# Queries projected by Wq times transposed Wk, formed on the chip, against unprojected keys: the mLSTM part of a hybrid encoder layer

## The chip, the cores and the metric

One Trainium2 chip, of which the kernel uses 1 core. The metric is the device time of one execution in microseconds (us), the median of several runs. The engines are PE (TensorE: PE the matmuls, PEld its weight loads), DVE (VectorE), ACT (ScalarE), POOL (GpSimd) and SP (SyncE, which issues most transfers). Each runs its own list of instructions in order; semaphores make one wait for another.

## The reference, cut to what matters

One encoder layer for 1024 tokens of width 1024, all float32. Two token mixers (a chunkwise mLSTM and an RG-LRU, each in two directions) run side by side, are merged by gates, and a product-key expert mixer (PEER) and a norm follow. The change touches the mLSTM alone, which has 4 heads of width 256:

```python
xc = silu(dwconv_centred(xm, conv_w, conv_b)).reshape(B, S, H, d)
q = einsum("bshd,hde->bhse", xc, w_q)
k = einsum("bshd,hde->bhse", xc, w_k) / sqrt(d)        # d = 256, so / 16
v = einsum("bshd,hde->bhse", xv, w_v)
# one direction, chunks of 128 tokens, carry (C, n, m):
s   = einsum("bhtd,bhsd->bhts", qc, kc) * w_intra
num = w_inter * einsum("bhtd,bhde->bhte", qc, C) + einsum("bhts,bhse->bhte", s, vc)
den = w_inter * einsum("bhtd,bhd->bht", qc, n) + sum(s)
kw  = kc * w_state
C   = decay * C + einsum("bhsd,bhse->bhde", kw, vc)
n   = decay * n + sum(kw)
```

The key k meets nothing but the query q: in the scores s, and through C and n, which are sums over keys. Nothing else reads either.

## The kernel before, in words

The work has these stages, by the clock of the profiled execution: the first norm, the projections and the RG-LRU (0 to about 397 us, the first mLSTM block among them), the four mLSTM heads one after the other (about 397 to 923 us), the merge of the two branches (923 to about 1100 us), the expert mixer's queries and its top-k searches (about 1100 to 1750 us), and then the dense stage with the gathers of expert rows (to the end). Products of two float32 values are mostly formed as three matmuls in the type float32r on split operands: `split` writes a high part (on ACT, line 78) and the remainder (on DVE or POOL, line 71), and `mm3` issues the three matmuls (lines 84, 85 and 86). A matmul of plain float32 tiles, without a split, shows in the trace as two PE records.

For one head the parts are these.

- `ml_x` projects two blocks of 128 channels, convolves them on DVE (line 321) and forms xc, which it splits into a high and a low tile.
- `ml_qkv` forms q and k: per head 2 x 2 x 2 groups of 6 matmuls 128x512 into a PSUM tile `pg`, each group moved out by one ACT activation (line 582). Its weights, 128x1024 with Wq in the left half and Wk in the right, come through a list of weight loads (`ws_plan`, `ws_get`): a raw tile `wr` (three buffers), a high tile `wh` from ACT and a low tile `wl` from POOL. Then it forms v in 48 matmuls 128x256.
- `ml_e` loads rows of exponents, masks them on POOL (line 619) and takes 16 exponentials on ACT (line 621).
- `ml_core` begins with the scores, plain float32 matmuls of k with q (line 638), and transposes of k (line 647). Then it works through 8 chunks in both directions; the states C and n go through DVE (line 685), ACT and POOL.
- `ml_out` normalises and transposes back (line 729), and multiplies into the gate tile on DVE (line 731).

Between the chunks of a head's core stand the projections that don't depend on it ("fill": the output gate of the head and the merge gates, 24 matmuls 128x512 per PSUM tile `ps`, with operand tiles `h`). Which instruction stands where on an engine is set by a scheduler that orders the program as it is built, by its own list of priorities; so a change in one place can move instructions in others.

SBUF tiles named `u` come from a pool of 18 tiles of 128x1032 float32; a name such as `u_2696` is a tile, `pg_2697` a PSUM tile, and the numbers run in order of their allocation.

Of the kernel before, what the change touches and what calls it, by code (L numbers as in the profile page):

```python
# [8 lines left out]
F32 = mybir.dt.float32  # L9
F32R = mybir.dt.float32r  # L10
# [3 lines left out]
AF = mybir.ActivationFunctionType  # L14
OP = mybir.AluOpType
# [7 lines left out]
H = 4  # L23
# [11 lines left out]
class K:  # L35
# [506 lines left out]
    def ml_x(self, h, done=None):  # L542

        nc = self.nc
        st = {}
        st["xm"], st["xc"] = [], []
        for e in range(2):
            blk = 2 * h + e
            x = self.pad_proj(blk, done if e == 0 else None)
            hi, lo = self.u(F32R), self.u(F32R)  # L550
            self.split(x[:, 2:2 + S], hi[:, :S], lo[:, :S])
            st["xm"].append((hi, lo))
            xc = self.u()
            self.conv(xc, x, V_MCW, V_MCB, blk)

            def act(xc=xc):
                nc.scalar.activation(xc[:, :S], xc[:, :S], AF.Silu)
                hi, lo = self.u(F32R), self.u(F32R)
                self.split(xc[:, :S], hi[:, :S], lo[:, :S])
                st["xc"].append((hi, lo))  # L560

            if e == 0:
                act()
            else:
                self.later = act
        return st

    def ml_qkv(self, h, st):
        nc = self.nc
        wh, wl = self.ws_get(("qk", h))  # L570
        for i, nm in enumerate(("q", "k")):
            st[nm] = []
            for e in range(2):
                t = self.u()
                for hf in range(2):
                    c = slice(hf * 512, hf * 512 + 512)
                    p = self.psg()
                    for cb in range(2):
                        o = i * 512 + cb * 256 + e * 128
                        self.mm3(p, (wh[:, o:o + 128], wl[:, o:o + 128]),  # L580
                                 (st["xc"][cb][0][:, c], st["xc"][cb][1][:, c]), cb == 0, cb == 1)
                    nc.scalar.activation(t[:, c], p, AF.Copy, scale=1.0 if i == 0 else 1.0 / 16.0)
                st[nm].append(t)
        wh, wl = self.ws_get(("v", h))
        st["v"] = []
        for g in range(2):
            vh, vl = (self.u(F32R).rearrange("p (c e) -> p c e", e=258) for _ in range(2))
            one = self.ones[:, 0:8].rearrange("p (c e) -> p c e", e=2)
            nc.gpsimd.tensor_copy(vh[:, :, 256:257], one[:, :, 0:1])
            self.sub("p", vh[:, :, 257:258], one[:, :, 0:1], one[:, :, 0:1])  # L590
            self.sub("p", vl[:, :, 256:258], one, one)
            for c in range(4):
                t = slice((g * 4 + c) * 128, (g * 4 + c) * 128 + 128)
                p = self.psg()
                for cb in range(2):
                    xh, xl = st["xm"][cb]
                    w = slice(cb * 256, cb * 256 + 256)
                    self.mm3(p[:, 0:256], (xh[:, t], xl[:, t]), (wh[:, w], wl[:, w]), cb == 0, cb == 1)
                nc.scalar.activation(vh[:, c, 0:256], p[:, 0:256], AF.Copy)
                self.sub("v", vl[:, c, 0:256], p[:, 0:256], vh[:, c, 0:256].bitcast(F32))  # L600
            st["v"].append((vh, vl))
        del st["xm"], st["xc"]
# [5 lines left out]
    def col(self, t, d, c, h):  # L608
        i = d * 32 + c * 4 + h
        return t[:, i:i + 1]  # L610
# [137 lines left out]
    def mixer_plan(self):  # L748
        plan = []
        inw = lambda b, e=WENG: plan.append((("in", b), [(self.A["win"][b], 1024)], 1024, e))  # L750
        lru = lambda n: plan.append((("lru", n), [(self.A["lwr"][n], 256), (self.A["lwi"][n], 256)], 512, "pd"))
        for n in range(NB + 1):
            if n == 1:
                lru(n - 1)
            inw(16 + n if n < NB else 0, "pd")
            if n in LRU_MG:
                inw(32 + LRU_MG.index(n))
            if n > 1:
                lru(n - 1)
            inw(24 + n if n < NB else 1, "pd")  # L760
            if n == 0:
                inw(48, "pd")
        seq = []
        mg = iter(range(len(LRU_MG), 16))
        m = lambda n: [("mg", next(mg)) for _ in range(n)]
        seq += m(MG[0])
        for h in range(H):
            for o in MLSEQ:
                if o == "m":
                    seq += m(1)  # L770
                elif o == "core":
                    seq += [(o, h)] + [m(1)[0] if f == "m" else ("o", h) for f in COREF[h]] + [("end", h)]
                elif o == "x":
                    seq += [("x", h + 1)] if h < H - 1 else m(LASTM)
                else:
                    seq += [(o, h)]
        seq += [("mg", i) for i in mg]
        for s_ in seq:
            if s_[0] == "x":
                inw(2 * s_[1])  # L780
                inw(2 * s_[1] + 1)
            elif s_[0] == "o":
                inw(8 + 2 * s_[1])
                inw(9 + 2 * s_[1])
            elif s_[0] == "mg":
                inw(32 + s_[1])
            elif s_[0] == "qkv":
                h = s_[1]
                plan.append((("qk", h), [(self.A["mwq"][h], 512), (self.A["mwk"][h], 512)], 1024, WENG))
                plan.append((("v", h), [(self.A["mwv"][h], 512)], 512, WENG))  # L790
        self.ws_plan(plan)
        self.seq = seq
# [741 lines left out]
WENG = "p"  # L1534
# [17 lines left out]
def host(**i):  # L1552
    f = lambda a: np.ascontiguousarray(a)
    a = {k: np.asarray(v) for k, v in i.items()}
    x = a["x"][0]
    d = {}
    d["xT"] = f(x.T.reshape(8, 128, S))
    w = a["w_in"][0]
    blk = lambda m: f(m.reshape(m.shape[0] // 128, 128, m.shape[1] // 128, 128).transpose(2, 1, 0, 3).reshape(
        m.shape[1] // 128, 128, m.shape[0]))  # L1560
    d["win"] = blk(np.concatenate([w[:, :2048], w[:, 2064:], w[:, 2048:2064], np.zeros((D, 112), np.float32)], axis=1))
    hw = lambda m: f(m[0].reshape(H, 2, 128, 256).transpose(0, 2, 1, 3).reshape(H, 128, 512))
    d["mwq"], d["mwk"], d["mwv"] = hw(a["mlstm_w_q"]), hw(a["mlstm_w_k"]), hw(a["mlstm_w_v"])
    lw = lambda m: f(m[0].transpose(1, 2, 0, 3).reshape(8, 128, 256))
    d["lwr"], d["lwi"] = lw(a["lru_w_r"]), lw(a["lru_w_i"])
    col = lambda v: v.reshape(-1, 128).T
    d["pvec"] = f(np.concatenate([
        col(a["norm1_g"][0]), col(a["mlstm_conv_w"][0]), col(a["mlstm_conv_b"][0]), col(a["mlstm_norm_g"][0]),
        col(a["lru_conv_w"][0]), col(a["lru_conv_b"][0]), col(a["lru_b_r"][0]), col(a["lru_b_i"][0]),
        col(a["lru_lambda"][0]), col(a["norm2_g"][0]),  # L1570
        np.concatenate([a["b_gates"][0], np.zeros(112, np.float32)])[:, None]], axis=1))
    d["bm"], d["bl"], d["wo"], d["wq"] = (blk(a[n][0]) for n in ("w_branch_mlstm", "w_branch_lru", "w_out", "peer_w_q"))
    d["keys"] = f(a["peer_sub_keys"][0].reshape(4, 4, 128, 128).transpose(0, 3, 1, 2).reshape(4, 128, 512))
    d["pu"], d["pv"] = f(a["peer_u"][0]), f(a["peer_v"][0])
    d["u5"] = f(a["peer_u"][0].reshape(128, 128, 8, 128).transpose(1, 3, 2, 0).reshape(128, 128, 1024))
    d["v5"] = f(a["peer_v"][0].reshape(128, 128, 1024).transpose(1, 0, 2))
    d["fg"] = f(a["final_norm_g"])
    d["g2"] = f(a["norm2_g"][0])
    return d
# [14 lines left out]
```

## Time and profile before

| what | value |
|---|---|
| median of 3 runs | 3574.14 us (3574.14, 3561.7, 3575.13) |
| the profiled execution, its own time | 3566.02 us |
| its span (first to last instruction) | 3563.9 us |
| mean granted TensorE clock, share of full speed | 0.969 |
| busy in the span | PE 94%, PEld 79%, DVE 82%, ACT 39%, POOL 48% |
| the four heads' stretch, 397 to 923 us | PE busy 484.5 of 526.0 us |

Every row of the trace is one execution's. A timeline row gives the start of a group of equal instructions and the time to the end of the last; matmuls overlap, so the cost of one in a row of many is the distance between starts, not the duration that stands beside it.

### The profile page before, as it was taken

Reading aid. Unit: us, or ns where it says so; the run is one execution under the profiler, and the core shown is the slowest. Engines: PE = TensorE matmul, PEld = TensorE weight load, DVE = VectorE, ACT = ScalarE, POOL = GpSimd, SP = SyncE. Lnnn points to the kernel's source line nnn. Section 1 sums busy time; section 2 is a strip of 40 time slices with the busy share of each in tenths; the row PEclk is TensorE's granted clock in tenths of the full one; section 3 lists DMA queues with packets and bytes.
Section 4 is the critical chain, followed back from the end, with each engine's and each line's share of the span. In section 5 each row is a group of like instructions: output and inputs, shape, how many; then the busy total and the mean of one; then the engine's idle time right before and its main releaser. Section 6 shows DMA issues by size and latency. Waiting matters only on the chain. (4 is left out here: it accounts for less than half of the span.)

```text
span 3563.9 us, 48538 instructions
## 1 busy us (share of the span) xinstructions
PE 3343.9 (94%) x17633; PEld 2827.0 (79%) x17633; DVE 2929.6 (82%) x5279; ACT 1392.0 (39%) x2565; POOL 1713.4 (48%) x1336
## 2 busy tenths in 40 slices
PE   7999999899899899878899999999999999999998
PEld 5787788778685565556788888998888999999987
DVE  8777574674327866998899999989999999999998
ACT  4565655655120240233333333343333334333333
POOL 7445354444102322342455555655555665666663
PEclk9999999999999999989899999999999999999999
DMA  2122211111466575558888879997887999999996
GB/s 107 60 71 68 72 51 51 63 48 44 154 217 208 159 251 199 174 170 258 312 318 301 283 275 342 360 338 276 314 284 279 341 357 351 344 347 334 352 348 239
DMA packets 319665, 812.56 MB, mean 228 GB/s; under 512 B 25600, under 2 KB 137408, under 8 KB 319424
## 3 DMA queue, kind: packets, MB, share of 16 engines
q0 software_dynamic: 115200, 419.48, 32.4%
q1 hardware_dynamic: 115184, 333.21, 26.7%
q10 hardware_dynamic: 89040, 56.76, 5.3%
q8 instruction: 138, 2.26, 0.3%
q14 instruction: 103, 0.84, 0.1%
HBM read 726.35 MB, written 83.00 MB: 227 GB/s over the span
## 5 line engine op out<-in xcount | busy, mean ns | idle before, releaser
L1334 POOL DMA_INDIRECT k<-in_pv,k x384 | 514.0, 1338 | 378.6 <-DVE k L1365 182.3
L1334 POOL DMA_INDIRECT k<-in_pu,k x384 | 506.6, 1319 | 332.7 <-DVE k L1357 148.0
L84 PE MATMUL ps<-h2h,wh 128*128 128x320 f32 x2048 | 637.2, 312 | 10.2 <-DVE u L1268 9.9
L85 PE MATMUL ps<-h2l,wh 128*128 128x320 f32 x2048 | 635.2, 310 | 0.0
L86 PE MATMUL ps<-h2h,wl 128*128 128x320 f32 x2048 | 628.9, 310 | 5.8 <-DVE wl L71 5.8
L851 PE MATMUL ps<-u,wr 128*128 128x384 f32 (+1 forms) x1920 | 581.1, 460 | 5.5 <-DMA u<-d 3.4
L1357 DVE SCALAR_TENSOR_TENSOR k<-k,rs,k 128x1024 f32<-128x1024 f32 x384 | 493.5, 1289 | 28.4 <-DMA k<-in_pu,k 28.4
L851 PEld LDWEIGHTS ps<-u,wr 128*128 128x128 f32 x1920 | 366.4, 194 | 181.7 <-issue 11.6
L85 PE MATMUL ps<-vl,wdh 128*128 128x512 f32 x1280 | 501.9, 393 | 2.5 <-DVE vl L71 2.5
L84 PE MATMUL ps<-vh,wdh 128*128 128x512 f32 x1280 | 469.0, 395 | 35.1 <-DVE u L1268 17.4
L1365 DVE SCALAR_TENSOR_TENSOR k<-k,k,k 128x1024 f32<-128x1024 f32 x384 | 494.6, 1288 | 0.4
L86 PE MATMUL ps<-vh,wdl 128*128 128x512 f32 x1280 | 494.3, 391 | 0.0
L84 PEld LDWEIGHTS ps<-h2h,wh 128*128 128x128 f32 x2048 | 388.1, 190 | 23.3 <-DVE u L1268 17.0
L86 PEld LDWEIGHTS ps<-h2h,wl 128*128 128x128 f32 x2048 | 385.6, 189 | 8.0 <-DVE wl L71 6.3
L85 PEld LDWEIGHTS ps<-h2l,wh 128*128 128x128 f32 x2048 | 387.8, 189 | 4.5
L1195 ACT ACTIVATE gel<-ps 128x320 f32<-128x320 f32 x256 | 111.1, 435 | 564.2 <-PE ps L86 549.4
L84 PEld LDWEIGHTS ps<-vh,wdh 128*128 128x128 f32 x1280 | 239.3, 189 | 88.2 <-DVE u L1268 22.5
L84 PE MATMUL ps<-h,wh 128*128 128x512 f32 x736 | 292.3, 399 | 14.0 <-ACT u L430 6.7
L86 PE MATMUL ps<-h,wl 128*128 128x512 f32 x736 | 290.8, 396 | 3.5 <-POOL wl L71 3.5
L85 PE MATMUL ps<-h,wh 128*128 128x512 f32 x736 | 291.0, 396 | 2.8 <-DVE h L253 2.8
L1238 ACT ACTIVATE gc<-gt 128x160 f32<-128x160 f32 x512 | 226.3, 510 | 155.9 <-DVE gel L1239 94.4
L86 PEld LDWEIGHTS ps<-vh,wdl 128*128 128x128 f32 x1280 | 241.4, 189 | 50.4
(327 smaller groups left out, 6079.1 us busy)
## 6 DMA issues: line engine op xcount, KB each, us to landing
wr<-in_u SPq DMA_DIRECT2D x128, 512.0 KB
wr<-in_v SPq DMA_DIRECT2D x128, 512.0 KB
d<-stg ACTq DMA_DIRECT2D x40, 1024.0 KB
gt<-d SPq DMA_DIRECT2D x64, 640.0 KB
wr<-in_win SPq DMA_DIRECT2D x49, 512.0 KB
wr<-in_wq SPq DMA_DIRECT2D x48, 512.0 KB
d<-u POOLq DMA_DIRECT2D x32, 512.0 KB
wr<-in_bm SPq DMA_DIRECT2D x24, 512.0 KB
```

The source lines that it names most:

```text
L84: mm(out, wh, mh, start=first, stop=False)
L85: mm(out, wh, ml, start=False, stop=False)
L86: self.lastmm = mm(out, wl, mh, start=False, stop=last)
L851: self.nc.tensor.matmul(p, w[:, cb * 128:cb * 128 + 128], m(cb), start=cb == 0, stop=cb == NB - 1)
L1195: nc.scalar.activation(gel[:, c], p, AF.Gelu)
L1238: nc.scalar.activation(gc[:, i * n:i * n + n], self.gt[j // 8, i][:, :, j % 8], AF.Copy)
L1334: nc.gpsimd.indirect_dma_start(out=t[:, :D], out_offset=None, in_=self.A["pu" if which == "u" else "pv"], in_offset=bass.IndirectOffsetOnA ...
L1357: nc.vector.scalar_tensor_tensor(r[:, :D], r[:, :D], self.rs2[:, b:b + 1], h2[:, :D], op0=OP.mult, op1=OP.mult, accum_out=dots[c][:, k % K ...
L1365: nc.vector.scalar_tensor_tensor(acc[:, :D], r[:, :D], ws[c][:, k % KB:k % KB + 1], acc[:, :D], op0=OP.mult, op1=OP.add)
```

## The change

The product of q and k is `xc Wq (xc Wk)^T / 16 = xc (Wq Wk^T / 16) xc^T`. The changed kernel forms the 256x256 matrix in brackets per head with 4 plain float32 matmuls 128x256 (line 576), from the raw weight tile, which now holds both matrices transposed by the host's layout. The result is split straight out of PSUM into one `u` tile, the high half by ACT (line 580) and the low half by DVE (line 581). The query is xc times that matrix: 24 matmuls 128x512 and 4 ACT activations (now line 592) per head. The key is xc itself, the unsplit tile of `ml_x`, which stays allocated for the core. The projection of k (24 matmuls, 4 activations) and the split of the 128x1024 weight tile (one ACT and one POOL instruction per head) are gone.

```diff
@@ ml_x
+                st["k"].append(xc)
@@ ml_qkv
-        wh, wl = self.ws_get(("qk", h))
-        for i, nm in enumerate(("q", "k")):
-            st[nm] = []
-            for e in range(2):
-                t = self.u()
-                for hf in range(2):
-                    c = slice(hf * 512, hf * 512 + 512)
-                    p = self.psg()
-                    for cb in range(2):
-                        o = i * 512 + cb * 256 + e * 128
-                        self.mm3(p, (wh[:, o:o + 128], wl[:, o:o + 128]),
-                                 (st["xc"][cb][0][:, c], st["xc"][cb][1][:, c]), cb == 0, cb == 1)
-                    nc.scalar.activation(t[:, c], p, AF.Copy, scale=1.0 if i == 0 else 1.0 / 16.0)
-                st[nm].append(t)
+        raw = self.ws_get(("qk", h))
+        p = self.psg()
+        for cb in range(2):
+            for eb in range(2):
+                nc.tensor.matmul(p[:, cb * 256:cb * 256 + 256], raw[:, eb * 256 + cb * 128:eb * 256 + cb * 128 + 128],
+                                 raw[:, 512 + eb * 256:512 + eb * 256 + 256], start=eb == 0, stop=eb == 1)
+        t = self.u(F32R)
+        wh, wl = t[:, 0:512], t[:, 512:1024]
+        nc.scalar.activation(wh, p, AF.Copy, scale=1.0 / 16.0)
+        nc.vector.scalar_tensor_tensor(wl, p, 1.0 / 16.0, wh.bitcast(F32), op0=OP.mult, op1=OP.subtract)
+        st["q"] = []
+        for e in range(2):
+            t = self.u()
+            for hf in range(2):
+                c = slice(hf * 512, hf * 512 + 512)
+                p = self.psg()
+                for cb in range(2):
+                    o = cb * 256 + e * 128
+                    self.mm3(p, (wh[:, o:o + 128], wl[:, o:o + 128]),
+                             (st["xc"][cb][0][:, c], st["xc"][cb][1][:, c]), cb == 0, cb == 1)
+                nc.scalar.activation(t[:, c], p, AF.Copy)
+            st["q"].append(t)
@@ mixer_plan
-                plan.append((("qk", h), [(self.A["mwq"][h], 512), (self.A["mwk"][h], 512)], 1024, WENG))
+                plan.append((("qk", h), [(self.A["mwq"][h], 512), (self.A["mwk"][h], 512)], 1024, None))
@@ the host's layout
-    d["mwq"], d["mwk"], d["mwv"] = hw(a["mlstm_w_q"]), hw(a["mlstm_w_k"]), hw(a["mlstm_w_v"])
+    ht = lambda m: hw(m.reshape(1, H, 256, 256).transpose(0, 1, 3, 2))
+    d["mwq"], d["mwk"], d["mwv"] = ht(a["mlstm_w_q"]), ht(a["mlstm_w_k"]), hw(a["mlstm_w_v"])
```

Lines behind the edit stand 10 or 11 further down in the changed file (582 of before is 592, 621 is 631, 638 is 648, 731 is 741).

PE's list at the first head, some 40 us ahead of its q, is one piece of the difference. The tiles `ps_2393` are of an input projection, `ps_2426`, `ps_2431` and `ps_2437` are gates of the RG-LRU, which read `u_2311` and `u_2312`.

```order
 L85 MATMUL ps_2393<-h_488,wh_2325 128x512
 L86 MATMUL ps_2393<-h_487,wl_2326 128x512
+L576 MATMUL pg_2692<-wr_2526 128x256 x2
 L84 MATMUL ps_2426<-u_2311,wh_2389 128x512
+L576 MATMUL pg_2692<-wr_2526 128x256
 L84 MATMUL ps_2431<-u_2311,wh_2389 128x512
-L84 MATMUL ps_2437<-u_2311,wh_2389 128x512
+L576 MATMUL pg_2692<-wr_2526 128x256
 L85 MATMUL ps_2426<-u_2312,wh_2389 128x512
 L86 MATMUL ps_2426<-u_2311,wl_2390 128x512
 L85 MATMUL ps_2431<-u_2312,wh_2389 128x512
 L86 MATMUL ps_2431<-u_2311,wl_2390 128x512
```

The four new matmuls of the first head are in the list before and between the first RG-LRU gate matmuls; the head's own q follows two `ps` tiles of fill later.

PE's list of the kernel before where q of the second head (`pg_4022`) begins, behind the last transposes of the first head's output:

```order
L729 MATMUL pg_3973<-c_89,u_2934 128x128
L729 MATMUL pg_3986<-c_89,u_2934 128x128
L84 MATMUL ps_4447<-h_444,wh_4228 128x512
L85 MATMUL ps_4447<-h_445,wh_4228 128x512
L84 MATMUL ps_4561<-h_444,wh_4228 128x512
L85 MATMUL ps_4561<-h_445,wh_4228 128x512
L84 MATMUL pg_4022<-u_3799,wh_3877 128x512
L85 MATMUL pg_4022<-u_3800,wh_3877 128x512
```

The same place in the changed kernel: the new matmuls into `pg_3987` stand behind the first matmul of the second fill tile, `ps_4501`, and q (`pg_3996`, with the matrix `u_3992`) behind its last.

```order
L86 MATMUL ps_4387<-h_487,wl_4169 128x512
L84 MATMUL ps_4501<-h_444,wh_4168 128x512
L576 MATMUL pg_3987<-wr_3776 128x256 x4
L85 MATMUL ps_4501<-h_445,wh_4168 128x512
...
L85 MATMUL ps_4501<-h_488,wh_4168 128x512
L86 MATMUL ps_4501<-h_487,wl_4169 128x512
L84 MATMUL pg_3996<-u_3769,u_3992 128x512
L85 MATMUL pg_3996<-u_3770,u_3992 128x512
```

So between the new matmuls and the first matmul of q that needs their result, 23 matmuls of fill stand; before, this fill stood behind and between the matmuls of q and k.

ACT's list of the changed kernel at the same place (`u_3959` and `u_3970` are the exponent tiles of `ml_e`, `wh_4618` and `wh_4383` the high parts of input weights):

```order
L78 ACTIVATE wh_4383<-wr_4166 128x1024
L631 ACT_TABLE_LOAD
L631 ACTIVATE u_3959<-u_3959,c_588 128x128 x8
L631 ACTIVATE u_3970<-u_3970,c_588 128x128 x8
L580 ACTIVATE u_3992<-pg_3987 128x512
L78 ACTIVATE wh_4618<-wr_4381 128x1024
L592 ACTIVATE u_3995<-pg_3996 128x512
```

The high half of the matrix (line 580) stands behind both batches of 8 exponentials; before, the first four activations of line 582 stood between the batches. Heads three and four read like the second. Behind the heads the two lists differ in places in the stretch from 1100 to 1750 us, where matmuls of the expert queries and of the one-hot selection are interleaved in another order (up to some 110 instructions further or nearer), and are the same in the dense stage.

## Rows read from the trace of the kernel before

**Rows 1.** The page: span, and busy time by engine.
```profile
span 3563.9 us, 48538 instructions
PE 3343.9 (94%) x17633; PEld 2827.0 (79%) x17633; DVE 2929.6 (82%) x5279; ACT 1392.0 (39%) x2565; POOL 1713.4 (48%) x1336
```
**Rows 2.** Windows: three stages, each engine's busy us (instructions), granted clock, DMA.
```profile
397.00:923.00 526.00, 484.51 (x2608) 416.21 (x2608) 322.70 (x739) 302.01 (x743) 235.82 (x267) 0.95 0.16 52
1100.00:1750.00 650.00, 564.58 (x2965) 382.30 (x2964) 552.67 (x1587) 168.49 (x315) 209.83 (x154) 0.93 0.65 209
1830.00:3564.00 1734.00, 1685.09 (x9337) 1524.46 (x9335) 1634.65 (x2335) 648.43 (x1152) 1017.07 (x759) 0.99 0.88 319
```
**Rows 3.** Windows inside the heads' stretch; columns PE, PEld, DVE, ACT, POOL.
```profile
410.00:510.00 100.00, 100.00 (x570) 87.74 (x569) 56.16 (x133) 56.09 (x143) 49.11 (x56) 1.00 0.17 48
510.00:530.00 20.00, 14.14 (x59) 11.93 (x58) 19.30 (x38) 12.97 (x28) 10.27 (x12) 0.66 0.20 65
550.00:640.00 90.00, 89.10 (x515) 78.17 (x514) 47.29 (x119) 46.51 (x118) 39.31 (x45) 1.00 0.12 39
```
**Rows 4.** Timeline of PE: the first score matmuls of the first two heads.
```profile
434.74 1.50 PE L638 MATMUL pg<-u,u 128*128 128x128 f32 x12
...
567.46 1.28 PE L638 MATMUL pg<-u,u 128*128 128x128 f32 x10
```
**Rows 5.** Timeline of PE: first of 24 q/k matmuls in a row, and the next behind.
```profile
417.52 0.40 PE L84 MATMUL pg<-u,wh 128*128 128x512 f32 x1
...
423.11 0.39 PE L84 MATMUL ps<-h,wh 128*128 128x512 f32 x1
```
**Rows 6.** Timeline of PE: the first and thirteenth of a run of 256-column matmuls.
```profile
562.09 0.28 PE L84 MATMUL pg<-wh,u 128*128 128x256 f32 x1
...
563.50 0.28 PE L84 MATMUL pg<-wh,u 128*128 128x256 f32 x1
```
**Rows 7.** Groups by line and form, 397 to 923 us: the score matmuls.
```profile
L638 PE MATMUL pg<-u,u 128*128 128x128 f32 x128 | 15.6, 275 | 0.0
```
**Rows 8.** Timeline of PE in the merge: 76 records of plain float32, 128x256.
```profile
983.76 16.57 PE L851 MATMUL ps<-u,wr 128*128 128x256 f32 x76
```
**Rows 9.** Timeline of PE ahead of the first head, idle time and releaser in brackets.
```profile
351.32 0.39 PE L86 MATMUL ps<-h,wl 128*128 128x512 f32 x1
356.24 0.80 PE L84 MATMUL ps<-u,wh 128*128 128x512 f32 x1 [4.54 <-ACT u L78]
358.15 0.80 PE L84 MATMUL ps<-u,wh 128*128 128x512 f32 x1 [1.11 <-ACT u L430]
...
396.98 0.50 PE L84 MATMUL pg<-u,wh 128*128 128x512 f32 x1 [2.94 <-ACT u L78]
398.24 0.78 PE L85 MATMUL pg<-u,wh 128*128 128x512 f32 x1 [0.76 <-DVE u L71]
...
404.58 0.50 PE L86 MATMUL ps<-h,wl 128*128 128x512 f32 x1 [1.03 <-POOL wl L71]
```
**Rows 10.** Timeline of ACT ahead of the first head.
```profile
396.83 1.07 ACT L332 ACTIVATE u<-ps 128x512 f32<-128x512 f32 x2
```
**Rows 11.** Groups by line and form, 397 to 923 us, of ACT, DVE and POOL.
```profile
L582 ACT ACTIVATE u<-pg 128x512 f32<-128x512 f32 x32 | 18.6, 593 | 15.2 <-PE pg L86 14.9
L641 DVE TENSOR_TENSOR u<-pg,u 128x512 f32<-128x512 f32 x16 | 10.3, 686 | 10.0 <-PE pg L638 10.0
L71 POOL TENSOR_TENSOR wl<-wr,wh 128x1024 fp32r<-128x1024 f32 x26 | 66.2, 2547 | 101.8 <-ACT wh L78 80.9 <-ACT s L78 7.5 <-PE pg L86 7.1
```
**Rows 12.** Timelines at the second head's q: PE's fill, POOL's mask, ACT's exponentials.
```profile
540.56 0.47 PE L84 MATMUL ps<-h,wh 128*128 128x512 f32 x1
...
543.29 2.42 POOL L619 TENSOR_TENSOR u<-u,c 128x1024 f32<-128x1024 f32 x1
...
548.16 2.44 ACT L621 ACTIVATE u<-u,c 128x128 f32<-128x128 f32 x8
```
**Rows 13.** Waits of PE, 923 to 1830 us: us in total, times, longest.
```profile
PE pg L1116 <- DVE g L1098: 26.7, 10, 4.4
```

More of the change, by code (lines that the diff above doesn't have):

```diff
@@ L545, in ml_x @@
         st = {}
-        st["xm"], st["xc"] = [], []
+        st["xm"], st["xc"], st["k"] = [], [], []
         for e in range(2):
```

## The prediction

> **What bounds the kernel now.** The page gives PE 94% of the span [rows 1]; the windows then show that the limits differ by stage [rows 2]. In the heads' stretch, where the change is, PE is busy 484.5 of 526.0 us and no other engine is above 323. From 1100 to 1750 us PE (565 of 650) and DVE (553) take turns, and in the dense stage both are nearly full. Inside the heads' stretch smaller windows show a repeating pattern [rows 3]: from 410 to 510 us and again from 550 to 640 us PE is busy all the time at full granted clock while DVE has half its time free; between them, from 510 to 530 us, DVE is full (19.3 of 20) and PE idles at a granted clock of 0.66. So each head is a long piece bound by PE, with q and k at its start, and a tail bound by the chain of DVE at the end of the core. The first score matmuls stand at 434.74 and 567.46 us, 132.7 us apart [rows 4]. What q and k cost is to be read in the piece bound by PE.
>
> Is PE full there, or only covered by overlapping records? Distances between starts answer: 24 matmuls of 512 columns from 417.52 to 423.11 us are 0.233 us each, and 12 of 256 columns from 562.09 to 563.50 us are 0.1175 [rows 5, 6]. Twice the columns take twice the time, without a fixed part, so PE streams at its rate and a matmul taken out gives back its whole distance. The Trainium skill (Perfetto Trace Analysis, Identifying the Most-Contended Engine) warns that busy time of matmuls is a bad measure of closeness to the roofline because they are pipelined, and names weight loads' busy share instead. By that, with PEld at 87.7 of 100 us in the first window, an eighth of each matmul taken out would be slack, and the sum below would be about 2 us smaller; the distances decide against it.
>
> **The change part by part.** *Taken off PE.* Per head 24 matmuls x 0.233 = 5.6 us [rows 5]. *Put on PE.* 4 plain float32 matmuls 128x256. The trace has this form in the merge: 76 records in 16.57 us, 0.218 each [rows 8], and two records make one matmul (128 records of the score line for 64 issued, [rows 7]), so 0.436 each and 1.75 us per head. Net 3.85 us per head.
>
> *First head.* The new matmuls stand ahead of the first RG-LRU gate matmul and behind its first ones. PE idles there 4.54 us until 356.24 for ACT's split and 1.11 us until 358.15 [rows 9]; two of them (0.87 us) fit in the first gap, and the rest nearly in the second. I charge 0.3 us. The q that stood at 396.98 us, behind an idle 2.94 us for xc's split, goes behind 48 fill matmuls. PE still waits there: the fill needs a PSUM tile that ACT empties at 396.83 [rows 10]. But the 0.76 us for DVE's low half and the 1.03 us for POOL's low weight half at 404.58 [rows 9] should go, since both have 11 us more. Against that 5 more fill matmuls stand ahead of the scores (1375 for 1370, counted in the lists), 1.1 us. Sum: 5.6 + 1.8 - 0.3 - 1.1 = 6.0, of which I keep 5.3 because some of the two waits can come back. The scores would begin at about 429.4 us. Bounds: 3.0 (new matmuls on the path, waits return) to 7.0.
>
> *Heads two to four.* Fill ahead of the scores is the same within one matmul, so the gain is the net 3.85, if PE does not wait. The new wait is PE's at q for DVE's line 581, behind ACT's line 580, behind both batches of exponentials. On before's clock POOL's second mask ends at 545.7, the second batch of 8 takes 2.44 us to 548.15 (ACT has nothing else there now), line 580, at line 582's 0.593 us, ends at 548.75 [rows 11, 12] and line 581 at 549.4 (nearest row: DVE from PSUM at this size, 0.686, [rows 11]). PE has 39 fill matmuls from 540.56 at 0.23 and 1.75 us of new ones: it comes to q at 551.2 [rows 12]. The slack is 1.8 us; heads three and four have the same order. So nothing is charged; without that cover the chain 0.6 + 0.7 and whatever ACT is late would be on the path. Line 581 stands on DVE behind the output multiply of the head before and needs nothing of q. Bounds for each: 0 to 4.2. I take 3.75.
>
> *Off the path.* Per head 4 ACT activations (2.4 us), one ACT and one POOL split of weights (2.55 us on POOL, [rows 11]) go; ACT and POOL have half of the stretch free [rows 2], so they count nothing, except that the next fill weights are split earlier. The raw weight tile is kept longer, one of three; xc's two tiles take the place of the two of k; the matrix is one more `u` tile for a short time. I find no transfer that this makes late, since the next two weight tiles are already loaded.
>
> *Tail and after.* The tail keeps its length and only starts earlier, since its chain begins when the core's chunks are done. The merge starts at once behind the last head. From 1100 to 1750 us the list is interleaved otherwise; PE waits 26.7 us for DVE's one-hot tiles alone in this part of the program [rows 13], and such waits could move by some 8 us either way, which I enter as spread and not as gain.
>
> Sum: 5.3 + 3 x 3.75 = 16.5 us. Against the profiled execution's 3566.0 that is 3549.5; the median of the runs shown is 3574.1, which gives 3557.6. I say 3556.
>
> **The rivals.**
> *The gain is lost in the tails.* If the chain of DVE and not PE's list set the end of each core, an earlier start would only lengthen PE's idle time from 510 to 530 us. For it: DVE's 19.3 of 20 us there. Against it: the chain's chunks alternate with fill in PE's own list, and DVE has 44% free from 410 to 510. Then only a third of the sum, some 5 us, would come out: 3569.
>
> *q waits for the matrix in each head (slower).* Place: the first matmul of q, in heads two to four. The matrix needs line 576, then ACT's line 580 at the end of 16 exponentials, whose masks wait for POOL. It eats the slack of 1.8 us first, and then 3.75 us of gain; if POOL's second mask comes more than about 5.5 us later than before, each head loses. One weight split of 2.5 us [rows 11] stands ahead of that mask; three more of them, or an equal stretch of other POOL work, would be 7.5 to 10 us of delay, and 10 us would make each head 4.5 us slower, together 13 less the first head's 5: 3582. For it: ACT's queue is in order and the exponentials have no reason to wait for PE. Against: POOL's load falls.
>
> *A luckier order.* If the second stretch's waits for one-hot tiles fall by a third (9 us) or the earlier split weights take PE's waits at the tails away (1 to 3 us per head), the gain is 25 to 28: 3548.
>
> *The change does not shorten the heads* because plain float32 matmuls cost far more in this place: they would have to cost 1.4 us each, three times the row, which I give no weight.
>
> **How the numbers follow.** Forecast as worked out 0.55, lost in the tails 0.14, q waits 0.09, luckier order 0.22. A 0.5% difference, 17.9 us, is about what a measurement of this kernel can tell from no change. The forecast lies just inside it; with the 8 us of spread about four in ten of its weight falls beyond, which with the luckier order makes faster 0.43, slower 0.07 and the same 0.50. The likeliest case's own range is 3547 to 3566; with the rivals the range is 3540 to 3573.
>
> **What would show it.** In the changed profile: the scores of the first two heads at about 429.4 and 558.4 us (before's less 5.3 and 9.05); between heads about 129 us; line 576 at 0.44 us per matmul; no wait of PE for line 581 over 1 us; PE busy in the stretch of the heads down by about 15 us, DVE as before; the merge 16 us earlier; from there to the end the same length within 8 us. Wrong would be: PE idle at q for DVE's line 581 or ACT's line 580; the distance between heads still 132 to 133; or a stretch 1100 to 1750 that differs by over 10 us.

## The result, and the profile after

The changed kernel takes 3535.24 us (median of 4 runs, 3533.16 to 3536.01), the kernel before 3574.64 us on the same chip (4 runs, 3561.7 to 3577.22): a ratio of 0.9896, 95% interval 0.9872 to 0.992. It is faster by 39 us, where 18 was predicted, and below the range. Its profiled execution took 3536.01 us. From profile to profile the span fell by 29.7 us, from 3563.9 [rows 1] to 3534.2; the other 9 us between the two differences are a matter of the kernel before, whose profiled execution (3566.02 us) lies that far below its median.

The page of the changed kernel, against [rows 1]: PE's busy time fell by 17 us, its share stayed.

```profile
span 3534.2 us, 48383 instructions
PE 3326.6 (94%) x17569; PEld 2816.7 (80%) x17569; DVE 2924.6 (83%) x5283; ACT 1381.9 (39%) x2549; POOL 1693.6 (48%) x1332
```

Windows of the changed kernel, with the columns of [rows 2]. The first is the heads' stretch, now from 397 to 902.9 us; the next two are the pieces of [rows 3] (the work there came 5 to 9 us forward, so that they are not quite the same). The last two go from one head's first score to the next head's, and serve an experiment below.

```profile
397.00:902.94 505.94, 468.84 (x2537) 405.57 (x2538) 327.75 (x742) 292.61 (x728) 224.80 (x262) 0.93 0.16 53
410.00:510.00 100.00, 97.31 (x558) 84.92 (x556) 59.38 (x140) 55.31 (x147) 51.87 (x59) 0.99 0.15 49
510.00:530.00 20.00, 16.34 (x57) 13.37 (x58) 19.46 (x37) 14.62 (x33) 7.40 (x8) 0.64 0.25 80
1100.00:1750.00 650.00, 576.37 (x3068) 399.52 (x3067) 553.86 (x1556) 180.50 (x334) 219.91 (x154) 0.94 0.68 221
...
429.45:558.47 129.02, 122.89 (x666) 106.90 (x665) 83.79 (x186) 74.78 (x183) 61.59 (x68) 0.93 0.18 60
558.47:687.84 129.37, 121.24 (x651) 104.89 (x650) 85.83 (x188) 74.80 (x183) 57.80 (x67) 0.92 0.18 56
```

In the heads PE was busy 15.7 us less than the 484.5 of [rows 2] and the stretch is 20.1 us shorter; the pattern of a full PE and a tail at the lower clock (0.64 from 510 to 530 us) is as before.

The timeline of the changed kernel. Line 576 forms the matrix, 580 and 581 split it, the `pg<-u,u` of line 84 is q, 648 the scores, 739 the transposes of the last head's output, 861 the merge's first matmuls.

```profile
429.45 1.95 PE L648 MATMUL pg<-u,u 128*128 128x128 f32 x16
...
536.51 0.48 PE L84 MATMUL ps<-h,wh 128*128 128x512 f32 x1
...
540.24 2.45 ACT L631 ACTIVATE u<-u,c 128x128 f32<-128x128 f32 x8 [2.33 <-POOL u L629]
540.25 1.89 PE L576 MATMUL pg<-wr 128*128 128x256 f32 x8
541.79 0.58 PE L85 MATMUL ps<-h,wh 128*128 128x512 f32 x1
542.20 0.40 PE L86 MATMUL ps<-h,wl 128*128 128x512 f32 x1
542.59 0.57 ACT L580 ACTIVATE u<-pg 128x512 fp32r<-128x512 f32 x1
543.20 0.69 DVE L581 SCALAR_TENSOR_TENSOR u<-pg,u 128x512 fp32r<-128x512 f32 x1 [4.97 <-ACT u L580]
547.21 0.40 PE L84 MATMUL pg<-u,u 128*128 128x512 f32 x1
...
558.47 1.95 PE L648 MATMUL pg<-u,u 128*128 128x128 f32 x16
...
687.84 1.95 PE L648 MATMUL pg<-u,u 128*128 128x128 f32 x16
...
816.70 1.95 PE L648 MATMUL pg<-u,u 128*128 128x128 f32 x16
...
899.01 3.93 PE L739 MATMUL pg<-c,u 128*128 128x128 f32 x16 [8.13 <-DVE u L733]
902.73 6.19 PE L861 MATMUL ps<-u,wr 128*128 128x256 f32 x24
...
1714.73 0.79 PE L84 MATMUL ps<-vh,wdh 128*128 128x512 f32 x1 [6.72 <-ACT wdh L78]
```

The first two heads' scores come 5.3 and 9.0 us earlier than in [rows 4], at the 429.4 and 558.4 forecast. The matrix is ready at 543.9 (line 581's end) and q begins at 547.2: 3.3 us of slack where 1.8 was reckoned. Both sides came earlier, with the whole first head: POOL's mask ends at 540.24, 5.5 us earlier than in [rows 12], and the second batch of exponentials follows at once; PE's 39 fill matmuls ahead of q begin 4.05 us earlier (536.51) and take with the new ones the 10.7 us that were reckoned. Between 540.25 and 542.20 stand four new matmuls and one of fill, 1.95 - 0.23 = 1.72 us, the 1.75 of the sum.

Waits of PE in the changed kernel: the heaviest from 395 to 905 us, and behind the "..." from 923 to 1830, where the first answers [rows 13].

```profile
PE pg L84 <- DVE s L695: 10.5, 8, 2.7
PE pg L739 <- DVE u L733: 8.1, 1, 8.1
PE ps L84 <- ACT u L332: 7.7, 4, 3.4
...
PE pg L1126 <- DVE g L1108: 31.0, 14, 5.0
PE pg L1089 <- DVE x L1085: 8.9, 2, 5.0
PE pg L1126 <- ACT stg L1129: 8.3, 3, 5.0
```

None is for line 580 or 581. The kernel before had there, beside [rows 13], these two:

```profile
PE pg L1079 <- DVE x L1075: 12.9, 2, 7.8
PE pg L1116 <- ACT stg L1119: 12.8, 4, 4.2
```

Where the 29.7 us came from is read from four more rows of the kernel before: the first scores of the third and fourth heads, the first matmul of the merge and the first of the dense stage.

```profile
700.72 1.05 PE L638 MATMUL pg<-u,u 128*128 128x128 f32 x8
...
834.75 1.05 PE L638 MATMUL pg<-u,u 128*128 128x128 f32 x8
...
923.25 7.03 PE L851 MATMUL ps<-u,wr 128*128 128x256 f32 x22 [1.31 <-DMA u<-d]
...
1742.86 0.80 PE L84 MATMUL ps<-vh,wdh 128*128 128x512 f32 x1 [8.81 <-ACT wdh L78]
```

The merge begins 20.5 us earlier (902.73), the dense stage 28.1 (1714.73), the end comes 29.7 earlier. So 20.5 came from the heads, 7.6 from the merge and the searches (819.6 us before, 812.0 now), 1.6 from the dense stage. That second term had no place in the sum.

### The profile page after: what moved, and what is told of

It reads as the page before. It is cut to its first block, busy times and chain, and to the rows that moved or that the text cites. A ratio compares the mean times of both kernels' runs of the same rounds, so it can differ in the third digit from the quotient of the medians.

```text
span 3534.2 us, 48383 instructions
## 1 busy us (share of the span) xinstructions
PE 3326.6 (94%) x17569; PEld 2816.7 (80%) x17569; DVE 2924.6 (83%) x5283; ACT 1381.9 (39%) x2549; POOL 1693.6 (48%) x1332
## 5 line engine op out<-in xcount | busy, mean ns | idle before, releaser
L85 PEld LDWEIGHTS ps<-vl,wdh 128*128 128x128 f32 x1280 | 241.8, 189 | 49.3 <-DVE vl L71 2.9
## 6 DMA issues: line engine op xcount, KB each, us to landing
gt<-d SPq DMA_DIRECT2D x64, 640.0 KB, 10.6
```

What stands on the lines that cost most here:

```text
L85: mm(out, wh, ml, start=False, stop=False)
```

## The experiments

**Heads and order, apart.** The theory after the result: the heads gave about 20 us, and the rest is the order that the scheduler wrote for the program behind the heads. The rival: that the later part gained because it starts earlier. From each kernel the list of every engine behind the last mixer was recorded, and in the other kernel each instruction was tied behind the one ahead of it in that list. The work behind the heads is the same in both kernels, and the lists hold the same instructions; PE's differ at 3094 of 12436 places, DVE's at 1381 of 3313. The section on the change says that the lists are the same in the dense stage. They are not: in the traces PE's matmuls stand in another order there too, up to about 2500 us. The heads' lists stayed as they were.

```diff
@@ behind the last instruction of the program
+        pin(tc, n0, ORDER)
@@ pin, for each engine's list
+        i = by[at]
+        if prev is not None:
+            tc.add_manual_dep(i, prev.name, mybir.DependencyInfo(
+                mybir.DependencyClass.NoSync, mybir.DependencyReason.DATA), reason="pin")
+        prev = i
```

The old heads with the changed kernel's later lists were to show:

> The four heads as in the kernel before, with all instructions behind the heads held in the order in which the changed kernel has them on each engine. Theory A (the order of the lists behind the heads gives some 14 us of the gain, the heads only what stands at their end): the heads end at 921 to 923 us as before, the merge takes its 96 us as before, and from 1018 us to the dense stage it is 14 us shorter; span about 3550 us, time 12 to 22 us below the kernel before. Rival B (the later stretch is shorter because the heads finish earlier and leave other buffers and transfers behind, the order doesn't matter): span within 4 us of 3564, ratio 0.998 to 1.001.

The new heads with the later lists of the kernel before:

> The changed heads, with all instructions behind the heads held in the order in which the kernel before has them. Theory A: the heads end at 902.7 us as in the changed kernel, the first part of the merge takes 4 us more than before, the stretch from there to the dense stage is as long as before (812 us); span about 3549 us, time about 15 us below the kernel before, 14 above the changed kernel's 3535. Rival B: time within 4 us of 3535.

Measured, against 3569.66 us of the kernel before (16 runs): old heads, new order 3558.41 (ratio 0.9965, 0.9953 to 0.9977); new heads, old order 3548.05 (0.9941, 0.9927 to 0.9955). So the order alone takes 11.3 us (8 to 17 by the interval), with no change in the heads, and the heads alone 21.6; together 32.9, where the changed kernel has 36 to 37 (below, 0.9898). The direction of both was forecast, the sizes (12 to 22 and about 15 us) were not met. Tying lists seems to cost little by itself, since it made the one kernel faster and the other slower by nearly the same (11.3, and 12 to 13). The timelines show the same direction. Old heads, new order: the merge starts where it did, the dense stage 9.5 us earlier. The dense stage itself takes 3.4 us longer, so that the span is only 6.1 us shorter (3557.8).

```profile
434.42 1.95 PE L638 MATMUL pg<-u,u 128*128 128x128 f32 x16
...
923.07 7.11 PE L851 MATMUL ps<-u,wr 128*128 128x256 f32 x24 [1.27 <-DMA u<-d]
...
1733.41 0.80 PE L84 MATMUL ps<-vh,wdh 128*128 128x512 f32 x1 [6.40 <-ACT wdh L78]
```

New heads, old order: from the merge's start to the dense stage 819.9 us, as before, in spite of the earlier start. So an earlier start alone doesn't shorten the later part, as the rival had it.

```profile
903.49 1.06 PE L861 MATMUL ps<-u,wr 128*128 128x256 f32 x4
...
1723.37 0.79 PE L84 MATMUL ps<-vh,wdh 128*128 128x512 f32 x1 [6.57 <-issue]
```

The waits of the old heads with the new order, from 923 to 1830 us:

```profile
PE pg L1116 <- DVE g L1098: 28.9, 14, 4.8
PE pg L1079 <- DVE x L1075: 8.8, 2, 4.9
...
PE pg L1116 <- ACT stg L1119: 4.9, 2, 3.3
```

The waits for the one-hot tiles, which the prediction watched, did not fall (26.7 to 28.9). Those that fell are PE's waits for the decoded indices (`x`, 12.9 to 8.8) and for the staging tiles that ACT empties (`stg`, 12.8 to 4.9). The first is 12.9 to 13.7 us in all four profiles with the old order and 7.9 to 9.1 in the eight others of this study, the second 10.6 to 12.8 and 4.9 to 9.3; that they go with the order is shown, that they are the whole of the 9 us is not. Nor is the order all: under the changed kernel's later lists the part from merge to dense stage took 805.5 to 818.1 us with the different heads of this study.

**q's columns put back.** What 24 matmuls of 128x512 cost in the heads' place: q's own are issued twice, the second set into a PSUM tile that nothing reads. In `k_columns_back` each group of 6 is issued again right behind its own activation, and the scheduler placed it; in `k_columns_pinned` all lists are the changed kernel's, with the 24 behind q's last. The edit shown is that of `k_columns_pinned`.

```diff
@@ ml_qkv, behind the loop that forms q
+        for e in range(2):
+            for hf in range(2):
+                c = slice(hf * 512, hf * 512 + 512)
+                p = self.psg()
+                for cb in range(2):
+                    o = cb * 256 + e * 128
+                    self.mm3(p, (wh[:, o:o + 128], wl[:, o:o + 128]),
+                             (st["xc"][cb][0][:, c], st["xc"][cb][1][:, c]), cb == 0, cb == 1)
```

> The changed kernel, with the 24 matmuls of q issued a second time per head into a PSUM tile that nothing reads (as many columns on TensorE as the projection of k had, without its evictions and without the split of its weights); what stands behind the heads keeps the changed kernel's order. Columns theory (each matmul in this stretch costs its 0.233 us on the path): 5.6 us per head, the last head's first scores at about 839 us instead of 816.7, time about 3557. Rival (the gain came from the evictions and weight splits taken off ScalarE and GpSimd): at most 1 us per head, time 3535 to 3539.

> The changed kernel with every engine's list held as it is there, and 24 more matmuls per head directly behind the last matmul of q, into PSUM tiles that nothing reads. Columns theory: 4 x 5.6 = 22.4 us and no more, heads ending at 925 us, time about 3557.5. If the extra 5 us of the earlier run with the same matmuls (heads ending at 930.1) was a price of the matmuls and not of lists that the scheduler ordered anew, it ends at 930 again, time 3563 or above.

They took 3568.82 us (against 3569.66: 0.9997, 0.9988 to 1.0006) and 3568.48 (against 3573.32 of 15 runs: 0.9985, 0.9976 to 0.9994), both some 11 us above the forecast of the columns theory. In `k_columns_back` the last head's scores stand at 844.1 us, for 839 forecast; in `k_columns_pinned` the heads end at 926.2, near the 925 of that theory. The scores of the pinned one:

```profile
437.31 1.95 PE L656 MATMUL pg<-u,u 128*128 128x128 f32 x16
...
572.25 1.95 PE L656 MATMUL pg<-u,u 128*128 128x128 f32 x16
...
706.13 1.95 PE L656 MATMUL pg<-u,u 128*128 128x128 f32 x16
...
840.58 1.95 PE L656 MATMUL pg<-u,u 128*128 128x128 f32 x16
```

Against the changed kernel they come 7.9, 13.8, 18.3 and 23.9 us later. The first of these holds a spread of 2.5 us (below); the distances between the heads grew by 16.0 in three, 5.3 each, and all four make 5.97 on the mean. By [rows 5] 24 x 0.233 = 5.6 each was due, and with an eighth of each matmul as slack, as the share of weight loads would have it, 4.9 each and 19.6 in all. The three distances grew by 5.9, 4.5 and 5.6: their mean lies between the two, nearer to 5.6, and doesn't decide between them. It does refute the rival, by which the gain had come from ACT and POOL (at most 1 us per head): the columns on PE cost what they were priced at, within a tenth on the mean. The miss is in the total: the pinned kernel is 33 us slower than the changed one by the medians (3535.92, below), not 24. With the changed kernel's lists it spends 818.1 us from merge to dense stage (`k_columns_back`: 814.7), between the two orders, and 5.6 us more in the dense stage. Why longer heads cost the later part more under the same lists stays open.

**The matrix earlier.** If line 576 stands on PE while PE waits anyway, its 1.75 us in heads two to four, 5.3 in all, should go. In `matrix_in_tail` it is formed in a step of its own just ahead of the next head's `ml_x`, at the end of the core, with its weight load; the lists behind the heads are the changed kernel's.

```diff
-    def ml_qkv(self, h, st):
+    def ml_mat(self, h):
...
+        self.mat = wh, wl
+
+    def ml_qkv(self, h, st):
+        nc = self.nc
+        wh, wl = self.mat
@@ the sequence of steps
-                    seq += [("x", h + 1)] if h < H - 1 else m(LASTM)
+                    seq += [("mat", h + 1), ("x", h + 1)] if h < H - 1 else m(LASTM)
+                elif o == "qkv":
+                    seq += [("mat", h), (o, h)] if h == 0 else [(o, h)]
```

> The changed kernel, with the matrix of heads two to four formed in the tail of the head before, where TensorE idles, instead of between the fill matmuls ahead of q; the rest behind the heads keeps the changed kernel's order. If the matrix costs its 1.75 us on the path where it stands and nothing in the tail: 3 x 1.75 us, time about 3530. Rival (the tail's idle time is only moved, or the matrix's tile held longer makes the next convolution wait): 3535 to 3540.

It took 3524.08 us (0.9875, 0.986 to 0.989, against 3569.66): 11 us less than the changed kernel by the medians, 8 by the two ratios, more than the 5.3 expected, and the fastest of all here with `tail_own_order`. Its windows from score to score, against the last two of the changed kernel's above:

```profile
430.31:556.16 125.85, 119.50 (x667) 103.87 (x666) 80.48 (x187) 74.18 (x185) 54.19 (x68) 0.99 0.18 57
556.16:681.36 125.20, 117.90 (x650) 103.06 (x648) 79.95 (x187) 74.07 (x184) 54.33 (x68) 0.96 0.18 57
```

The heads are 3.2 and 4.2 us shorter with as many PE instructions. Over the three windows PE is idle 21.1 us, where it was 22.7 and 24.9 in the two profiles of the changed kernel: the waits that the new matmuls were to fill gave some 2 to 4 of the 11 us by which the three windows are shorter, for 5.3 expected. PE is busy 355.1 us for 364.6 and 362.4, and the granted clock is 0.99 and 0.96 in the two rows for 0.93 and 0.92. A window's mean clock doesn't tell its length, though: in the second profile of the changed kernel the second window has 0.95 for 0.92 and is as long, 129.2 us. It matters where the clock is low. Four rows show it: that window, then ten us behind the second head's tail, where PE is full, in the changed kernel's first and second profile and in `matrix_in_tail`.

```profile
555.60:684.80 129.20, 119.54 (x650) 103.43 (x649) 85.85 (x188) 74.96 (x183) 58.29 (x67) 0.95 0.19 56
...
649.00:659.00 10.00, 10.00 (x35) 8.01 (x34) 9.75 (x16) 8.49 (x23) 3.22 (x2) 0.74 0.64 140
646.00:656.00 10.00, 10.00 (x35) 7.95 (x35) 9.83 (x16) 8.48 (x23) 3.23 (x2) 0.75 0.71 141
636.00:646.00 10.00, 10.00 (x46) 8.26 (x45) 8.77 (x17) 8.31 (x22) 0.00 (x0) 1.00 0.11 39
```

Both profiles of the changed kernel get through 35 matmuls there, `matrix_in_tail` through 46. A dozen fill matmuls begin 0.43 us apart at the lower of the clock's two levels (0.50, 1.2 GHz) instead of 0.23, which is 2.4 to 2.6 us in that head; in `matrix_in_tail` none does. In the ten us ahead PE had been busy 6.1 us in the first profile of the changed kernel, and 8.5 in `matrix_in_tail`.

DVE differs too. The first two rows here are of the changed kernel, the third of `matrix_in_tail`:

```profile
523.61 6.01 DVE L321 SCALAR_TENSOR_TENSOR u<-u,c,u 128x1024 f32<-128x1024 f32 x3
524.14 3.01 POOL L629 TENSOR_TENSOR u<-u,c 128x1024 f32<-128x1024 f32 x1
...
527.73 3.99 DVE L321 SCALAR_TENSOR_TENSOR u<-u,c,u 128x1024 f32<-128x1024 f32 x3
```

Three steps of the convolution take 6.01 us with a mask of POOL beside them and 3.99 without, 2.0 us more in each head, and DVE's chain bounds the tail. Neither difference was tested by itself, so what each gives of the 11 us is not shown.

The order of the tail changed too: some 55 fill matmuls that stood between scores and transposes now stand behind them. `conv_behind_core` tests whether the place of the next head's convolution on DVE did that, in the changed kernel without moving the matrix: it ties the split and convolution of `ml_x` behind DVE's last instruction of the core.

```diff
@@ ml_x, around the split and around the convolution
+            with self.tc.issue_after(self.coredve.ins) if h else ExitStack():
```

> The changed kernel with the split and the convolution of the next head queued on VectorE behind the last instruction of the head's core; the matrix stays between the fill ahead of q. In the run with the matrix in the tail the lists had changed in this way too, and it gained 11 us where the matrix alone was worth 5.3. If that rest is the order on VectorE: 4 to 7 us below the changed kernel, time 3528 to 3531. If the whole gain there was the matrix's place: no change, 3533 to 3538.

It took 3543.47 us (0.9928, 0.9914 to 0.9942), slower than the changed kernel, its heads 131.7 to 133.2 us apart:

```profile
426.90:558.58 131.68, 117.54 (x659) 102.11 (x658) 81.57 (x186) 72.85 (x183) 54.26 (x67) 0.96 0.17 55
558.58:691.34 132.76, 118.63 (x651) 103.47 (x649) 84.57 (x187) 74.06 (x184) 54.25 (x67) 0.92 0.17 54
```

PE is busy as little as in `matrix_in_tail`, but idle 14.1 us of each. The steps of the convolution are the short ones here too (1.28 us each). So the convolution behind the core is not what made `matrix_in_tail` faster, and how far the clock behind the tail and the steps without a mask beside them did, stays open.

**A third pair for the order.** `matrix_in_tail` once with the later lists of the kernel before, once with those that its own scheduler writes; the edit is the pin as above, or none.

> The kernel with the matrix in the tail (3524.1 us with the changed kernel's lists behind the heads), now with the lists of the kernel before behind the heads: the third pair that differs in nothing else. The two pairs so far gave 11.3 and 12 to 13 us. Order theory: 11 to 13 us slower, 3535 to 3537. If the stretch behind the heads follows from how the heads end and the two pairs were chance: 3522 to 3527.

> The same heads, with the lists behind them as the scheduler orders them for this kernel itself: a third order. Order theory makes no forecast beyond its spread, 3518 to 3540; a value equal to 3524 within 2 us would say that the scheduler's orders mostly agree and the kernel before had an unlucky one.

Against 3571.42 us (9 runs) they took 3538.13 (0.9914, 0.99 to 0.9928) and 3525.33 (0.9866, 0.9847 to 0.9884): the old order costs 14.0 us against `matrix_in_tail`, the pair that was planned, and 12.8 against its own order, in the same series. From the merge's start to the dense stage it takes 825.2 us, for 811.8 with its own order and 805.5 in `matrix_in_tail`. By the spans of the single profiles the three pairs differ by 6.1, 7.1 and 15.9 us, so the size of the effect is known less well than the medians make it look. The own order lies within 2 us of 3524, which was to mean that only the kernel before had an unlucky one; its four runs spread over 16 us (3515.62 to 3531.46), so that is not shown.

**Both kernels once more.** The spread had to be known.

> The changed kernel again, beside the runs of this call: 3533 to 3538 us, heads ending at 902 to 904 us. If it came out near 3545, part of what was put down to the order of the lists would have been the chip's difference.

> The kernel before, a second profile, to see which stage its own spread of 3562 to 3577 us comes from. If the stretch behind the heads: heads ending at 921 to 922 us again whatever the time; if the heads: their end moves with the time.

The changed kernel took 3535.92 us (3532.56 to 3537.85; 0.9898, 0.9882 to 0.9913), its heads ending at 900.3 us, earlier than expected; the profile of the kernel before 3564.33 us in its one run, while its 15 timed runs in the same series had a median of 3573.32. Its merge begins at 923.08 us, where it did, and its time is that of the first profile, so which stage makes the spread stays open. In the second profile of the changed kernel the first scores stand here:

```profile
426.92 1.95 PE L648 MATMUL pg<-u,u 128*128 128x128 f32 x16
```

That is 2.5 us earlier than in the first, so a start of the heads is known to about 2.5 us; the distances between heads agree within 0.6.

## Why the prediction was right or wrong

**What bounds the heads** was read rightly. The 24 matmuls cost about their distances in the piece bound by PE (5.3 us on the mean of three heads, 5.6 by the rows), a new plain float32 matmul costs 0.43, and the heads follow at 129 us. The share of weight loads, which the Trainium skill (Perfetto Trace Analysis, Identifying the Most-Contended Engine) prefers to busy time of matmuls, would have made it 4.9. The single heads measured 4.5 to 5.9, so "the distances decide against it" is more than the runs show.

**The sum of the heads**, 16.5 us, was somewhat small: 20.5 by the traces. The first three heads' scores came 5.3, 9.0 and 12.9 us earlier (5.3, 9.05 and 12.8 by the working); the fourth gave 5.2 and not 3.75, because before, the third and fourth heads stood 134.0 us apart, and the first two 132.7 [rows 4]; the last tail and the merge's start gave another 2.5. That the first head's 5.3 came out to the tenth is partly luck, since a start has a spread of 2.5 us (in the second profile of the changed kernel it is 7.8).

**q does not wait for the matrix**, as said, and with more slack, since the masks moved forward with the first head by more than PE's fill did. From a head's scores to the transposes of its output it takes 103.2 to 105.4 us, for 103.5 to 104.9 before: the tails did not take up the gain, so that rival fell too.

**The step that failed** is this: "From 1100 to 1750 us the list is interleaved otherwise; PE waits 26.7 us for DVE's one-hot tiles alone in this part of the program [rows 13], and such waits could move by some 8 us either way, which I enter as spread and not as gain." The new interleaving was worth 11 to 14 us by the medians in three pairs of kernels with equal heads, and 7.6 us from merge to dense stage in the two profiles compared here. That a profile of the kernel before could have given the sign is not shown; but the rows beside [rows 13] had the two waits that moved, 25.7 us together, and the text looked only at the one-hot tiles, which stayed. The rival of a luckier order was the nearest in size, with a gain of 25 to 28 us, and named the wrong wait.

**The base.** The sum was taken from the median of the runs and worked out on the profiled execution, as if the two differed by a constant. They don't: the kernel before is 3564 to 3566 us in both profiles and 3570 to 3575 in its medians, and the difference lies in no trace that was taken. `new_heads_old_order` shows it too (profiled 3543.1, median 3548.05), `tail_old_order` doesn't. So of the 39 us by medians, 20.5 are the heads and 9.2 what stands behind them (7.6 of it up to the dense stage) by the traces; the last 9 to 10 are measured but not placed.

## What to carry to other kernels

Price an instruction in a stretch bound by PE by the distance between starts: it came out within some 10% on the mean of three heads, and within 20% in each. When a scheduler writes the lists, a local edit also rewrites lists far away, and that can be worth half as much as the edit or more: compare the lists, name each wait in the stretch that is rewritten, and when measuring, tie the later lists to one order, so that edit and order are seen apart. A short producer that one long consumer needs is worth trying in the tail ahead of it: it took another 8 to 11 us here, of which the reason expected gives 2 to 4.

## What the runs showed of the hardware that was not expected

The same kernel reached the first scores at 429.45 and at 426.92 us in two profiles; the heads then ran alike, 129 us each. And a head's mean granted clock did not tell its length: at 0.92 and at 0.95 the second window of the changed kernel took 129.4 and 129.2 us, PE being busy 121.2 and 119.5, while behind the tail, where PE is full, both had 0.74 to 0.75 and 35 matmuls in ten us, and `matrix_in_tail` 1.00 and 46. Three DVE instructions of 128x1024 took 6.01 us beside one of POOL of the same size and 3.99 without it.
